# Attention of a two-layer diffusion backbone: heads paired within a key/value head, and single-pass products of split probabilities with split values

## The chip, the cores and the metric

The kernel runs on one core of one Trainium2 chip. The metric is the device time of one execution in microseconds (us); the times given are medians over runs. TensorE is called PE here, VectorE DVE, ScalarE ACT, GpSimd POOL; PEld is TensorE's weight load.

## What is computed

The reference runs two layers over 512 latent tokens and 256 context tokens of width 1024. A layer normalizes, projects, runs three token mixers (attention, pooling, Fourier mixing), gates and sums them, projects again, and ends with a gated MLP. The change is in the attention, which has 8 query heads of width 64 over 2 key/value heads:

```python
def latent_attention(q, k, v, kc, vc, sink):
    qb = q.reshape(B, nb, BLOCK, N_KV_HEADS, Q_PER_KV, HEAD_DIM)
    kb, vb = band(k), band(v)
    s_lat = jnp.einsum('bnqhgd,bnkhd->bhgnqk', qb, kb) * scale
    s_lat = jnp.where(valid, s_lat, NEG_INF)
    s_ctx = jnp.einsum('bnqhgd,bchd->bhgnqc', qb, kc) * scale
    p = jax.nn.softmax(jnp.concatenate([s_lat, s_ctx, sink_column(...)], -1))
    o = (jnp.einsum('bhgnqk,bnkhd->bnqhgd', p_lat, vb)
         + jnp.einsum('bhgnqc,bchd->bnqhgd', p_ctx, vc))
```

A block of 128 latent queries sees its own block of keys and its neighbours, and all 256 context keys; context queries (in the first layer alone) see the context keys. Query head h uses key/value head h // 4.

## The kernel before

All activations lie transposed: channels on the 128 partitions, tokens along the free axis, columns 0 to 511 latent (`LS`), 512 to 767 context (`CS`). Weights come as 128x1024 tiles (`wraw`), which ACT rounds to a float32r part `whi` (L323) and DVE reduces to the rest `wlo` (L324). Every large product is made of three float32r products of 128x128 weights with up to 512 columns (`mmk`, L346), into PSUM banks called `mp` and `mm`.

The attention stage works on a pair of heads `t` (0 to 3) and a block `n` of 128 queries: 24 such units in the first layer (6 blocks, two of them of context queries), 16 in the second. A pair is one head of each key/value head, t and 4 + t, so that its two halves of 64 channels lie on partitions 0 to 63 and 64 to 127. A unit has two halves of code:

- `scores` (L587 to L637): for each head h, PE multiplies the queries with the two parts of the keys (`ka`, `kb`, float32r, 256 or 384 columns, L602 to L607) and adds the masks (L614) in a PSUM tile `sc`; DVE takes the maximum (L617), ACT the exponential into `p` (L627), DVE divides by the sum (L634).
- `pv` (L638 to L662): PE transposes the probabilities in blocks of 128x128 (L649) into the one PSUM bank `tp`, up to four blocks of one head at a time; ACT or DVE, in turn, copies the bank to `pt` (L651, L653). Then each 128-key chunk is multiplied: the weights are 64 columns of the values `vs` in float32, the moving side 128 columns of `pt`, one product for each head at its own column half of the array (`tile_position`, L658), both into one bank `pv`. ACT copies the result to `o` (L662).

A unit has 4 or 5 chunks (latent blocks at the edge, inside) or 2 (context blocks): 160 chunks in all, 88 in the first layer and 72 in the second, so 320 transposes and 320 products at L658; the trace has two records for each of these float32 products, 640.

The kernel is written so that unit n + 1's `scores` comes before unit n's `pv`. After every third unit (second in the second layer) `filler` multiplies one part of the Fourier branch and its gates (L346), work that attention doesn't need. At the middle of the stage the queries of heads t = 2, 3 are projected (`attn_q`). A scheduler then sets each engine's fixed order from this program, so fillers stand between the steps of a unit; engines run their order in sequence and wait on semaphores.

`attn_kv` (L562 to L584) makes the keys' parts and the values: it transposes the values in 128-token chunks (L582) and ACT copies them into the float32 tile `vs` (L583). `SBB` (L36) gives the buffers of the stage's temporary tiles.

Of the kernel before, what the change touches and what calls it, by code (L numbers as in the profile page):

```python
# [35 lines left out]
SBB = dict(p=2, pt=3)  # L36
# [85 lines left out]
class Kern:  # L122
# [52 lines left out]
    def tmp(self, tag, w=N):  # L175
# [7 lines left out]
        return self.tp.tile([P, w], F32, tag=tag, name=tag, bufs=self.sbt[tag])  # L183
# [379 lines left out]
    def attn_kv(self, l, hs, ls, streams):  # L563
# [14 lines left out]
        vs = self.slot(F32)  # L578
        for c0, c1 in (LS, CS):
# [3 lines left out]
            nc.scalar.copy(vs[:, c0 : c1], pv)  # L583
        return ka, kb, vs  # L584

    def scores(self, l, t, n, qs, ka, kb):
# [11 lines left out]
        for h in range(2):  # L598
# [3 lines left out]
            nc.tensor.matmul(cx, q, ka[h][:, T : N], start=True, stop=False)  # L602
            nc.tensor.matmul(cx, q, kb[h][:, T : N], start=False, stop=True)
            if bl:
                bd = s[:, 0:bl]
                nc.tensor.matmul(bd, q, ka[h][:, k0 : k0 + bl], start=True, stop=False)  # L606
                nc.tensor.matmul(bd, q, kb[h][:, k0 : k0 + bl], start=False, stop=False)  # L607
# [30 lines left out]
    def pv(self, st, vs, o):  # L638
        nc = self.nc
        pr, chunks, q0 = st  # L640
        nch = len(chunks)
        pts = []
        for h in range(2):
            pt = self.tmp("pt", 640)
            for j0 in range(0, nch, 4):
                j1 = min(j0 + 4, nch)
                tpb = self.bk("tp", (j1 - j0) * P)
                for j in range(j0, j1):
                    nc.tensor.transpose(tpb[:, (j - j0) * P : (j - j0 + 1) * P], pr[h][:, j * P : (j + 1) * P], self.ident)  # L649
                if (h + j0 // 4) % 2 == 0:  # L650
                    nc.scalar.copy(pt[:, j0 * P : j1 * P], tpb)  # L651
                else:
                    nc.vector.tensor_copy(pt[:, j0 * P : j1 * P], tpb)  # L653
            pts.append(pt)
        po = self.bk("pv", P)
        for j, c in enumerate(chunks):
            for h in range(2):
                nc.tensor.matmul(  # L658
                    po[64 * h : 64 * h + 64, :], vs[:, c * P + 64 * h : c * P + 64 * h + 64],
                    pts[h][:, j * P : (j + 1) * P], start=(j == 0), stop=(j == nch - 1), tile_position=(0, 64 * h),  # L660
                )
        nc.scalar.copy(o[:, q0 : q0 + P], po)  # L662

    def layer(self, l, xs, streams, h=None, after=None):
# [112 lines left out]
        for half in range(2):  # L777
# [3 lines left out]
            for t in ts:  # L781
                for n in range(nblk):
                    st = (self.scores(l, t, n, qs[t], ka, kb), o[t])
# [309 lines left out]
```

## Time and profile before

| | before |
|---|---|
| median of 3 runs | 1896.56 us (1896.4 to 1897.75) |
| span of the profiled execution | 1894.8 us |
| around it (median less span) | 1.8 us |
| PE busy | 1848.8 us, 98% of the span |
| DVE, ACT, POOL busy | 1222.7 us (65%), 679.4 us (36%), 143.2 us (8%) |
| attention, first layer | 205 to 402 us |
| attention, second layer | 1257 to 1399 us |
| granted TensorE clock, both stages | 1.00, which is 2.4 GHz |

The profile is one execution. Busy time is the share in which an engine works on something; PE's records overlap, since a product's end is modelled behind its start, so what a product costs PE is the distance from its start to the next one's start, and not its length. The stages of attention are the stretches in which the names `sc`, `tp`, `pt` and `pv` stand in the trace.

### The profile page before, as it was taken

To read this page: it belongs to the slowest core of one execution; us is meant where nothing else is said; L and a number is where in the kernel's file an instruction comes from. 1 tells how busy PE (TensorE), PEld (TensorE's weight loads), DVE (VectorE), ACT (ScalarE), POOL (GpSimd) and SP (SyncE) were. 2 spreads that over 40 slices of the span, in tenths; PEclk is the share of its full clock that TensorE was granted. 3 is DMA by queue.
4 is the path that set the end of the run, shared out by engine and by line. 5 is a ranking of instruction groups with operands and counts; after the bars stand their busy time and mean duration, and the time that the engine had idled before them with its cause. 6 is when DMAs were issued, how large, how long until landed. Compare 5 with 4: busy or idle time off the path is not lost. (4 is left out here: it accounts for less than half of the span.)

```text
span 1894.8 us, 26908 instructions
## 1 busy us (share of the span) xinstructions
PE 1848.8 (98%) x10584; PEld 1569.8 (83%) x10584; DVE 1222.7 (65%) x2313; ACT 679.4 (36%) x1132; POOL 143.2 (8%) x102
## 2 busy tenths in 40 slices
PE   6999999999999999999999999999999999999997
PEld 4888877788888888888888888877778988888887
DVE  5687655557758995757566676556753776556556
ACT  4332444432234331313232234344443444233333
POOL 2000101012100000000000031010112200000003
PEclk8999999999999999999999999999999999999998
DMA  9244101024542442323233343321123623222233
GB/s 358 90 143 146 46 23 56 23 74 142 169 150 99 147 132 80 122 89 123 89 123 100 111 146 101 104 78 46 51 70 100 203 91 99 95 99 96 99 99 114
DMA packets 75998, 205.09 MB, mean 108 GB/s; under 512 B 8288, under 2 KB 15712, under 8 KB 75744
## 3 DMA queue, kind: packets, MB, share of 16 engines
q1 hardware_dynamic: 75872, 203.38, 33.1%
q8 instruction: 83, 1.36, 0.3%
q14 instruction: 43, 0.35, 0.1%
HBM read 199.15 MB, written 4.19 MB: 107 GB/s over the span
## 5 line engine op out<-in xcount | busy, mean ns | idle before, releaser
L346 PE MATMUL mm<-slot,whi 128*128 128x512 f32 (+1 forms) x3468 | 895.8, 348 | 7.7 <-DVE slot L886 2.7
L346 PEld LDWEIGHTS mm<-slot,whi 128*128 128x128 f32 x3468 | 609.0, 191 | 89.6 <-DVE slot L886 3.1
L346 PE MATMUL mp<-slot,whi 128*128 128x512 f32 (+1 forms) x2404 | 643.8, 353 | 3.0 <-ACT tg L525 1.5
L346 PE MATMUL mm<-slot,wlo 128*128 128x512 f32 (+1 forms) x1734 | 600.2, 346 | 0.0
L346 PEld LDWEIGHTS mp<-slot,whi 128*128 128x128 f32 x2404 | 418.3, 189 | 64.3 <-issue 6.6
L323 ACT CAST whi<-wraw 128x1024 fp32r<-128x1024 f32 x260 | 272.7, 1049 | 539.2 <-PE mm L346 309.4
L324 DVE TENSOR_TENSOR wlo<-wraw,whi 128x1024 fp32r<-128x1024 f32 x245 | 304.3, 1242 | 246.4 <-ACT whi L323 238.7
L346 PE MATMUL mp<-slot,wlo 128*128 128x512 f32 (+1 forms) x1202 | 421.5, 351 | 1.0 <-POOL wlo L324 1.0
L346 PEld LDWEIGHTS mm<-slot,wlo 128*128 128x128 f32 x1734 | 330.9, 191 | 40.1 <-DVE wlo L324 0.6
L346 PEld LDWEIGHTS mp<-slot,wlo 128*128 128x128 f32 x1202 | 227.4, 189 | 31.8 <-issue 4.3
L294 DVE SCALAR_TENSOR_TENSOR junk<-wmod,cb 128x512 f32<-128x512 f32 x256 | 177.4, 693 | 7.8 <-DMA wmod<-in_w_mt_dram 3.8
L886 DVE SCALAR_TENSOR_TENSOR slot<-mm,mod,slot 128x512 f32<-128x512 f32 (+1 forms) x109 | 66.8, 616 | 62.7 <-PE mm L346 62.7
L324 POOL TENSOR_TENSOR wlo<-wraw,whi 128x1024 fp32r<-128x1024 f32 x15 | 36.8, 2455 | 878.8 <-ACT whi L323 878.8
L532 POOL TENSOR_TENSOR slot<-slot,tg 128x512 f32<-128x512 f32 (+1 forms) x48 | 62.2, 1296 | 408.7 <-DVE tg L531 375.8
L835 DVE SCALAR_TENSOR_TENSOR cp<-mm,p,cp 128x511 f32<-128x511 f32 (+2 forms) x122 | 79.2, 650 | 17.5 <-ACT cp L834 15.6
L627 ACT ACTIVATE p<-sc,sm 128x512 f32<-128x512 f32 (+2 forms) x80 | 54.9, 687 | 32.7 <-PE tp L649 21.0
L658 PE MATMUL pv<-pt,slot 128*64 128x128 f32 x640 | 64.3, 283 | 0.4
L834 ACT ACTIVATE cp<-mm,p 128x512 f32<-128x512 f32 (+1 forms) x60 | 36.8, 613 | 57.6 <-PE mm L346 57.6
L617 DVE TENSOR_REDUCE sm<-sc 128x1 f32<-128x512 f32 (+2 forms) x80 | 53.5, 683 | 6.0 <-PE sc L614 6.0
L658 PEld LDWEIGHTS pv<-pt,slot 128*64 128x64 f32 x640 | 41.2, 136 | 17.8 <-issue 8.2
L653 DVE COPY pt<-tp 128x512 f32<-128x512 f32 (+2 forms) x56 | 30.1, 537 | 39.6 <-PE tp L649 39.5
L649 PE MATMUL tp<-p,p 128*128 128x128 f32 x320 | 54.7, 277 | 0.9 <-ACT pt L651 0.9
(157 smaller groups left out, 1323.8 us busy)
## 6 DMA issues: line engine op xcount, KB each, us to landing
wraw<-in_w_up_dram SPq DMA_DIRECT2D x88, 512.0 KB, 3.5
wmod<-in_w_mt_dram SPq DMA_DIRECT2D x160, 256.0 KB, 3.0
wraw<-in_w_in_dram SPq DMA_DIRECT2D x68, 512.0 KB, 3.5
wraw<-in_w_dn_dram SPq DMA_DIRECT2D x56, 512.0 KB, 3.4
wraw<-in_w_out_dram SPq DMA_DIRECT2D x32, 512.0 KB, 3.5
slot<-in_w_m_dram SPq DMA_DIRECT2D x20, 384.0 KB, 7.5
wraw<-in_w_bra_dram SPq DMA_DIRECT2D x8, 512.0 KB, 3.6
slot<-in_xc_dram SPq DMA_DIRECT2D x8, 256.0 KB, 4.5
```

Of the source, the lines that this page charges most:

```text
L294: nc.vector.scalar_tensor_tensor(junk[:, 0:512], w, 1.0, self.cb[:, b, hs], ALU.mult, ALU.mult, accum_out=acc[:, b * 2 + h : b * 2 + h + 1])
L323: self.cpy = nc.scalar.copy(hi, raw)
L324: (eng or nc.vector).tensor_tensor(lo, raw, hi.bitcast(F32), ALU.subtract)
L346: self.mm = self.nc.tensor.matmul(out, ww, xx, start=(k == 0 and i == 0), stop=(k == n - 1 and i == 2))
L532: nc.gpsimd.tensor_tensor(y[:, c0 : c1], y[:, c0 : c1], tg[:, c0:c1], ALU.add)
L617: nc.vector.tensor_reduce(mx[:, h : h + 1], s, AX.X, ALU.max)
L627: nc.scalar.activation(p[:, :w], ps[h], AF.Exp, bias=ngm[:, h : h + 1], scale=0.125, accum_out=den[:, h : h + 1])
L649: nc.tensor.transpose(tpb[:, (j - j0) * P : (j - j0 + 1) * P], pr[h][:, j * P : (j + 1) * P], self.ident)
L658: nc.tensor.matmul(po[64 * h : 64 * h + 64, :], vs[:, c * P + 64 * h : c * P + 64 * h + 64], pts[h][:, j * P : (j + 1) * P], start=(j == 0 ...
L834: nc.scalar.activation(c[:, c0:c1], ps, AF.Copy, scale=cw(1))
L835: tap = lambda d, src, i: nc.vector.scalar_tensor_tensor(c[:, d], src, cw(i), c[:, d], ALU.mult, ALU.add)
L886: nc.vector.scalar_tensor_tensor(xv, ps, g2(m, b), xv, ALU.mult, ALU.add)
```

## The change

Heads are paired as 2t and 2t + 1, which share one key/value head (`t // 2`), so one unit needs one head's values alone. `attn_kv` makes for each key/value head a float32r tile with, per chunk, 128 columns: the values rounded to float32r (64 columns) and the rest (64 columns). `pv` transposes two chunks of both heads at a time into the bank `tp` (512 columns); ACT rounds the bank to `ph` (float32r), and DVE then subtracts that from the bank to get `pl`. A chunk's values are the weights of two products of 256 columns (both heads), one with `ph`, one with `pl`, in one bank of 128 x 256. The two halves of its partitions, the products with the two parts of the values, are added at the end: for each head ACT copies one half to `o` and DVE adds the other.

```diff
-SBB = dict(p=2, pt=3)
+SBB = dict(p=3, ph=2, pl=1)
...
     def attn_kv(self, l, hs, ls, streams):
...
-        vs = self.slot(F32)
+        vs = self.slots(2)
         for c0, c1 in (LS, CS):
...
-            nc.scalar.copy(vs[:, c0 : c1], pv)
+            src = pv.rearrange("p (c d) -> p c d", d=P)
+            for h in range(2):
+                dst = vs[h][:, c0:c1].rearrange("p (c d) -> p c d", d=P)
+                own = src[:, :, 64 * h : 64 * h + 64]
+                nc.scalar.copy(dst[:, :, 0:64], own)
+                nc.vector.tensor_tensor(dst[:, :, 64:P], own, dst[:, :, 0:64].bitcast(F32), ALU.subtract)
...
     def scores(self, l, t, n, qs, ka, kb):
-            nc.tensor.matmul(cx, q, ka[h][:, T : N], start=True, stop=False)
+            nc.tensor.matmul(cx, q, ka[t // 2][:, T : N], start=True, stop=False)
...
     def pv(self, st, vs, o):
         pr, chunks, q0 = st
         nch = len(chunks)
-        pts = []
+        po = self.bk("pv", 2 * P)
+        for j0 in range(0, nch, 2):
+            j1 = min(j0 + 2, nch)
+            w = (j1 - j0) * 2 * P
+            tpb = self.bk("tp", w)
+            for j in range(j0, j1):
+                for h in range(2):
+                    x = ((j - j0) * 2 + h) * P
+                    nc.tensor.transpose(tpb[:, x : x + P], pr[h][:, j * P : (j + 1) * P], self.ident)
+            hi, lo = self.tmp("ph", 512, F32R), self.tmp("pl", 512, F32R)
+            nc.scalar.copy(hi[:, :w], tpb)
+            nc.vector.tensor_tensor(lo[:, :w], tpb, hi[:, :w].bitcast(F32), ALU.subtract)
+            for j in range(j0, j1):
+                v = vs[:, chunks[j] * P : (chunks[j] + 1) * P]
+                x = (j - j0) * 2 * P
+                nc.tensor.matmul(po, v, hi[:, x : x + 2 * P], start=(j == 0), stop=False)
+                nc.tensor.matmul(po, v, lo[:, x : x + 2 * P], start=False, stop=(j == nch - 1))
         for h in range(2):
-            pt = self.tmp("pt", 640)
-            for j0 in range(0, nch, 4):
...
-        po = self.bk("pv", P)
-        for j, c in enumerate(chunks):
-            for h in range(2):
-                nc.tensor.matmul(
-                    po[64 * h : 64 * h + 64, :], vs[:, c * P + 64 * h : c * P + 64 * h + 64],
-                    pts[h][:, j * P : (j + 1) * P], start=(j == 0), stop=(j == nch - 1), tile_position=(0, 64 * h),
-                )
-        nc.scalar.copy(o[:, q0 : q0 + P], po)
+            own, oth = (slice(0, 64), slice(64, P)) if h == 0 else (slice(64, P), slice(0, 64))
+            dst = o[own, q0 : q0 + P]
+            nc.scalar.copy(dst, po[oth, h * P : (h + 1) * P])
+            nc.vector.tensor_tensor(dst, po[own, h * P : (h + 1) * P], dst, ALU.add)
...
-heads = np.array([[t, 4 + t] for t in range(4)]).reshape(-1)
```

On the host the heads' columns in the weights are no longer permuted (the last lines of the diff), which moves no instruction. Outside the attention stages PE, POOL and SP have the same instructions in the same order.

In the first layer, PE's order in the middle of a unit of 5 chunks stood before as below (`tp` transposes, `pv` products with the values, `mp` fillers):

```order
L649 MATMUL tp<-p_87,p 128x128 x4
L346 MATMUL mp<-slot,whi 128x256
L346 MATMUL mp<-slot,wlo 128x256
L346 MATMUL mp<-slot,whi 128x512 x2
L649 MATMUL tp<-p_87,p 128x128
L658 MATMUL pv<-pt,slot 64x128
L346 MATMUL mp<-slot,wlo 128x512
L346 MATMUL mp<-slot,whi 128x512
L649 MATMUL tp<-p_87,p 128x128 x4
```

The same place in the changed program:

```order
L655 MATMUL tp<-p_87,p 128x128 x4
L662 MATMUL pv<-ph,slot 128x256
L663 MATMUL pv<-pl,slot 128x256
L662 MATMUL pv<-ph,slot 128x256
L663 MATMUL pv<-pl,slot 128x256
L655 MATMUL tp<-p_87,p 128x128 x4
L346 MATMUL mp<-slot,whi 128x256 x2
L346 MATMUL mp<-slot,wlo 128x256
```

The products are now of 128 weights and 256 columns, in twos per chunk. In the whole program the 320 products with the values stood in 96 runs between other work of PE: 56 of a single product, 8 of three, 16 of seven and 16 of eight. They now stand in 154 runs, still 320 products.

At the end of the second layer's attention PE's order was:

```order
L649 MATMUL tp<-p_87,p 128x128 x4
L658 MATMUL pv<-pt,slot 64x128
L346 MATMUL mp<-slot,whi 128x512 x2
L346 MATMUL mp<-slot,wlo 128x512
L346 MATMUL mp<-slot,whi 128x512
L658 MATMUL pv<-pt,slot 64x128 x7
L346 MATMUL mp<-slot,whi 128x512
```

It is now:

```order
L655 MATMUL tp<-p_87,p 128x128 x7
L662 MATMUL pv<-ph,slot 128x256
L663 MATMUL pv<-pl,slot 128x256
L662 MATMUL pv<-ph,slot 128x256
L663 MATMUL pv<-pl,slot 128x256
L655 MATMUL tp<-p_87,p 128x128
L662 MATMUL pv<-ph,slot 128x256
L663 MATMUL pv<-pl,slot 128x256
```

The fillers have moved ahead: from the last scores to the stage's end PE now has only transposes (18, of five groups) and products with the values, and the following projections come after the last product.

On DVE, one unit in the middle of the second layer now reads (`pl` is the new subtraction, L668 the new addition, L622 the maximum, L639 the division):

```order
L658 TENSOR_TENSOR pl<-tp,ph 128x256
L622 TENSOR_REDUCE sm_12075<-sc 128x1
L626 SCALAR_TENSOR_TENSOR sm_12090<-sm_12075,nsink 128x2
L668 TENSOR_TENSOR slot<-pv,slot 64x128
L628 TENSOR_TENSOR sm_12092<-sm_12090,nsink 128x2
L658 TENSOR_TENSOR pl<-tp,ph 128x512
L668 TENSOR_TENSOR slot<-pv,slot 64x128
L324 TENSOR_TENSOR wlo<-wraw,whi 128x1024
L658 TENSOR_TENSOR pl<-tp,ph 128x512
```

Before, the same unit had two copies, of 128x128 and of 128x512, where three subtractions and two additions now stand; over the program DVE has 88 subtractions and 80 additions in place of 56 copies, and ACT 88 roundings and 80 copies in place of 96 copies.

## Rows read from the trace of the kernel before

**Rows 1.** The page: busy time of each engine, and the chain that ended last by engine.

```profile
PE 1848.8 (98%) x10584; PEld 1569.8 (83%) x10584; DVE 1222.7 (65%) x2313; ACT 679.4 (36%) x1132; POOL 143.2 (8%) x102
...
PE 27%; DVE 1%; issue 1%; ACT 0%; POOL 0%; POOLq 0%; DVEq 0%; ACTq 0%
```

**Rows 2.** Busy time in the two attention stages: us, then each engine's busy us (instructions).

```profile
205.00:402.00 197.00, 193.08 (x1315) 152.04 (x1313) 113.88 (x270) 86.19 (x219) 19.54 (x18) 1.00 0.11 35
1257.00:1399.00 142.00, 139.96 (x906) 106.08 (x907) 98.12 (x196) 67.24 (x155) 16.62 (x11) 1.00 0.15 48
```

**Rows 3.** PE's waits in the first layer's stage: us in total, times, longest.

```profile
PE mp L346 <- ACT tg L525: 1.5, 6, 0.3
PE sc L602 <- ACT p L627: 1.2, 2, 0.7
```

**Rows 4.** PE's timeline around a single product: start us, length us, what.

```profile
229.86 0.27 PE L649 MATMUL tp<-p,p 128*128 128x128 f32 x1
230.07 0.43 PE L658 MATMUL pv<-pt,slot 128*64 128x128 f32 x2
230.43 0.50 PE L346 MATMUL mp<-slot,wlo 128*128 128x512 f32 x1
230.76 0.39 PE L346 MATMUL mp<-slot,whi 128*128 128x512 f32 x1
```

**Rows 5.** PE's timeline around scores and four transposes.

```profile
227.66 0.28 PE L602 MATMUL sc<-slot 128*128 128x256 f32 x1
227.78 0.28 PE L603 MATMUL sc<-slot 128*128 128x256 f32 x1
227.90 0.28 PE L606 MATMUL sc<-slot 128*128 128x256 f32 x1
...
228.50 0.60 PE L649 MATMUL tp<-p,p 128*128 128x128 f32 x4
228.85 0.48 PE L346 MATMUL mp<-slot,whi 128*128 128x512 f32 x1
229.17 0.39 PE L346 MATMUL mp<-slot,wlo 128*128 128x512 f32 x1
229.40 0.63 PE L346 MATMUL mp<-slot,whi 128*128 128x512 f32 x2
```

**Rows 6.** PE's timeline around a run of eight products (16 records).

```profile
1390.46 0.33 PE L649 MATMUL tp<-p,p 128*128 128x128 f32 x1
1390.72 1.09 PE L658 MATMUL pv<-pt,slot 128*64 128x128 f32 x16
1391.74 0.74 PE L346 MATMUL mp<-slot,whi 128*128 128x512 f32 x2
1392.32 0.39 PE L346 MATMUL mp<-slot,wlo 128*128 128x512 f32 x1
```

**Rows 7.** ACT's and DVE's copies of the transposes, by shape; DVE's small addition nearest in shape.

```profile
L651 ACT COPY pt<-tp 128x512 f32<-128x512 f32 x32 | 18.8, 586 | 48.4 <-PE tp L649 48.3
L651 ACT COPY pt<-tp 128x256 f32<-128x256 f32 x8 | 3.0, 373 | 7.4 <-PE tp L649 7.4
...
L653 DVE COPY pt<-tp 128x512 f32<-128x512 f32 x32 | 22.1, 690 | 28.5 <-PE tp L649 28.4
L653 DVE COPY pt<-tp 128x256 f32<-128x256 f32 x8 | 3.4, 422 | 4.8 <-PE tp L649 4.8
...
L514 DVE TENSOR_TENSOR cp<-aux,st 128x128 f32<-128x128 f32 x3 | 0.9, 286 | 0.0
```

**Rows 8.** Timeline: the copy behind the transposes of rows 5; ACT handing to DVE.

```profile
229.13 0.59 ACT L651 COPY pt<-tp 128x512 f32<-128x512 f32 x1 [1.66 <-PE tp L649]
...
468.99 0.84 ACT L350 CAST slot<-slot 128x768 fp32r<-128x768 f32 x1 [1.69 <-POOL slot L532]
...
469.86 0.96 DVE L351 TENSOR_TENSOR slot<-slot 128x768 fp32r<-128x768 f32 x1 [0.34 <-ACT slot L350]
```

More of the change, by code (lines that the diff above doesn't have):

```diff
@@ L173, in aux, with tmp @@
         return self.bk("aux", w)
-    def tmp(self, tag, w=N):
+    def tmp(self, tag, w=N, dt=F32):
         if tag == "tg":
@@ L182, in tmp @@
             tag = "cv"
-        return self.tp.tile([P, w], F32, tag=tag, name=tag, bufs=self.sbt[tag])
+        return self.tp.tile([P, w], dt, tag=tag, name=tag, bufs=self.sbt[tag])
     def small(self, w):
@@ L601, in scores @@
             cx = s[:, bl:w]
-            nc.tensor.matmul(cx, q, ka[h][:, T : N], start=True, stop=False)
-            nc.tensor.matmul(cx, q, kb[h][:, T : N], start=False, stop=True)
+            nc.tensor.matmul(cx, q, ka[t // 2][:, T : N], start=True, stop=False)
+            nc.tensor.matmul(cx, q, kb[t // 2][:, T : N], start=False, stop=True)
             if bl:
                 bd = s[:, 0:bl]
-                nc.tensor.matmul(bd, q, ka[h][:, k0 : k0 + bl], start=True, stop=False)
-                nc.tensor.matmul(bd, q, kb[h][:, k0 : k0 + bl], start=False, stop=False)
+                nc.tensor.matmul(bd, q, ka[t // 2][:, k0 : k0 + bl], start=True, stop=False)
+                nc.tensor.matmul(bd, q, kb[t // 2][:, k0 : k0 + bl], start=False, stop=False)
                 ms = []
@@ L782, in layer @@
                 for n in range(nblk):
-                    st = (self.scores(l, t, n, qs[t], ka, kb), o[t])
+                    st = (self.scores(l, t, n, qs[t], ka, kb), vs[t // 2], o[t])
                     if prev:
-                        self.pv(prev[0], vs, prev[1])
+                        self.pv(*prev)
                     prev = st
@@ L789, in layer @@
                         filler()
-            self.pv(prev[0], vs, prev[1])
+            self.pv(*prev)
         for _ in range(8):
@@ L1044, in _layout @@
             poolw[o : o + 64, l, g // 2, o : o + 64] = i["pool_w"][l, g]
-    heads = np.array([[t, 4 + t] for t in range(4)]).reshape(-1)
-    sink = np.broadcast_to(i["attn_sink"][:, heads].reshape(1, 16), (P, 16))
+    sink = np.broadcast_to(i["attn_sink"].reshape(1, 16), (P, 16))
     a["pk2"] = np.concatenate(
@@ L1064, in _layout @@
     a["w_brp"], a["w_brf"] = two(i["w_br_pool"]), two(i["w_br_four"])
-    wa = tile_m(i["w_br_attn"][:, qp], 4, 8)
+    wa = tile_m(i["w_br_attn"], 4, 8)
     a["w_bra"] = wa.reshape(NL, 4, 2, P, 4, P).transpose(0, 1, 3, 2, 4, 5).reshape(NL, 4, P, 1024)
```

12 lines of the change are left out of this document (1 added, 11 removed).

## The prediction

> **What bounds the kernel now.** The page comes first: PE is busy for 98% of the span and holds 27 of the 30% of the span that the chain of waits names [rows 1]. What changes lies in two stages, so I read those alone. In both PE is busy for 98% of the stretch, DVE for 58% and 69% [rows 2], and PE's list of waits over the first stage's 197 us holds 2.7 us in these two lines [rows 3]. So both stages last as long as PE's own list of work, and the first question is what that list gets shorter by. The second is whether DVE and ACT still deliver in time when it is shorter.
>
> **What a product with the values costs PE today.** I read distances between starts. Take a single product, in two records: from the transpose at 229.86 to the second filler at 230.76 are 0.90 us [rows 4]. In them lie one transpose and one 512-column filler. That filler costs 0.23 elsewhere (229.17 to 229.40), and four transposes with one filler take 0.67 (228.50 to 229.17), so a transpose costs 0.11 [rows 5]. The single product is left with 0.56 us. Its two records account for 0.22 at a transpose's rate, so 0.34 is a fixed toll of going into this kind of product and out again. For a run of eight (16 records) from 1390.46 to 1392.32 are 1.86 us; less one transpose and two fillers that is 1.29 [rows 6]. There two records, one of each column half, go at a time. A run of three then costs 0.34 + 4 x 0.11 = 0.78; runs of seven have one unpaired product and I price them as runs of eight.
>
> The order has 56 runs of one, 8 of three, 32 of seven or eight: 31.4 + 6.2 + 41.3 = **78.9 us**, of which 44.8 fall to the first layer (32, 8 and 16 runs) and 34.1 to the second (24 and 16).
>
> **What it costs afterwards.** 320 products of 128 weights and 256 float32r columns, the shape of the scores, whose starts lie 0.12 apart [rows 5]: 320 x 0.12 = **38.4 us**. I charge no toll on entering them, because a filler behind transposes pays none: 4 x 0.11 + 0.23 is all that rows 5 leave. The transposes are the same 320. PE's list shortens by **40.5 us**, 23.7 in the first layer and 16.8 in the second.
>
> The Trainium skill, page TensorEngine Tiling (Array Packing), section Key Properties, speaks against the change: different column tiles work in parallel. By that rule alone, with a chunk's four records in 4 x 0.11 / 2 = 0.22 us, 160 chunks cost 35.2 us before and 38.4 afterwards, and the sum would be 3 us slower; rows 6 show the pairing, rows 4 show that 56 products have no partner beside them and that each run pays 0.34.
>
> **What is added elsewhere.** DVE loses 56 copies (30.1 us; 25.5 of them in the two larger shapes [rows 7]). It gets 88 subtractions from PSUM, 72 of 512 and 16 of 256 columns, at the copies' 0.69 and 0.42 [rows 7]: 56.4 us. It also gets 80 additions of 64 x 128 at the 0.29 of the nearest small operation on PSUM [rows 7]: 22.9 us. Net 49, split by chunks 27 and 22. The stages' DVE work goes from 114 and 98 us [rows 2] to 141 and 120. Against stages of 197 - 24 = 173 and 142 - 17 = 125 us that is 81% and 96%: DVE is no longer idle enough to be ignored. ACT gets 88 roundings and 80 copies for 96 copies, some 20 us in the first stage: 106 of 173. The values' preparation in `attn_kv` adds four DVE and two ACT operations per layer of under half a microsecond each; the first scores and the fillers ahead of the first products hide them, and without that cover it would be 2 us.
>
> **What the new hand-overs cost.** There is still one bank `tp`, and a group of transposes is now read by ACT, then by DVE, before PE may write the next. From a group's first transpose to ACT's start are 0.63 us (228.50 to 229.13), ACT takes 0.59, the hand-over to DVE 0.03 (469.83 to 469.86), DVE 0.69, and PE is back 0.14 after a copy's end (229.72 to 229.86) [rows 4, 5, 7, 8]: **2.08 us** for four transposes with idle queues, 1.37 for two. What stands in PE's order within that time hides it.
>
> At the end of the second layer's attention nothing does: five groups (four of four, one of two) take 4 x 2.08 + 1.37 = 9.7 us, and PE has 18 transposes and 18 products for it, 4.1 us. It waits **5.6 us**. Before, fillers stood there, as the order shows.
>
> Elsewhere I went along the new order with these prices and wrote down how much less than the need stands between a group and the product or transpose that waits for it. Most loops hold 2 to 4 us of PE work and cover it. Where the order excerpt shows four transposes, four products and four transposes again, 0.92 us stand against 2.08, and the products themselves wait. All such places together make **9.1 us**.
>
> The last term is unknown: a subtraction may find DVE at other work. At 82% busy and 0.42 us a DVE instruction (113.88 / 270 [rows 2]), a chance arrival waits 0.17; on ACT, 0.6 x 0.39 / 2 = 0.11. Counted along the same order, 0.28 us more on each group lengthens PE's list by 10.6 us, about 43% of 88 x 0.28, because the rest finds cover. Bounds: 0 where the subtractions meet an idle DVE, as most copies do now, and 18 us where DVE's queue makes the delay half a microsecond. I take **7**, nearer the chance arrival, since DVE's order puts most of the subtractions between short instructions.
>
> **Sum.** -40.5 + 5.6 + 9.1 + 7 = -18.8 us. The profiled execution has a span of 1894.8 and some 1.8 around it, which is the median of the runs, 1896.56; the forecast is 1896.6 - 18.8 = **1878 us**. A measurement of this kernel can tell a change of about 0.2%, 4 us, from none.
>
> **Rivals.**
>
> *DVE's and ACT's queues become the bound; slower.* Its place is the bank `tp`, one group after another. Each 0.1 us of mean delay per group costs PE 3.8 us at first and over 4 later on; with 14.7 us already gone to waits, the gain is used up at about 0.6 us of delay, and at 0.66, where the waits come to 45 us, the time is **1901**. For it: in the second stage 96% of DVE would be needed at PE's pace. It has additions that wait for ACT's copies ahead of subtractions that PE waits for, and today's tolls on PE give DVE and ACT time that disappears. Against it: a stage that waits gets longer, so DVE's share falls (at 137 us to 88%), which limits the delay; and today DVE sits idle for 28.5 us ahead of its 32 larger copies [rows 7], so most of them find it free. 10%. The Trainium skill, same page, section PSUM Bottleneck, states this case: more speed on TensorE does not speed up emptying PSUM, which can become the limit. No row of the kernel before shows that limit reached.
>
> *The toll stays.* If the 0.34 us came with the change of bank or operand rather than with column halves, 154 runs would pay 52 us, and the products would cost 91: 12 us more than now, **1909** before any wait. Transposes and score products change bank and operand too and pay nothing [rows 5], so 3%. The same section Key Properties has a rule on this side: a change of tiling mode drains the array; by it the toll goes.
>
> *All hand-overs covered but the tail.* Then 40.5 - 5.6 = 34.9 us are won: **1862**. For it: PE's list of waits is short today [rows 3]. Against: the copies there are one step, not two. 17%.
>
> *Won and lost in equal parts,* with 0.5 to 0.65 us of delay per group and a time within 4 us of today's. 8%.
>
> The forecast, a gain of 8 to 30 us, has 62%. The range from 1862 to 1898 leaves out most of the two slower rivals and half of the full gain. Faster: 62 + 17 = 79%; the same 8%; slower 13%.
>
> **What would show it.** In the trace of the changed kernel: products with the values 0.12 apart with no gap behind transposes (else the toll stays); `tp` bank cycles near 2.1 us and PE waiting at the new subtraction's products by 10 to 25 us over the two stages; the first stage 10 to 16 us shorter, the second 3 to 9; DVE near 77% and 88% of the stages; the tail of the second layer with PE idle about 6 us. The forecast is wrong if a stage is longer than before, if PE waits under 8 us or over 35, or if time moves outside the two stages.

## The result, and the profile after

The changed kernel takes **1912.1 us** (median of 4 runs, 1910.9 to 1913.7) against 1896.9 for the kernel before on the same chip: ratio 1.0078, 95% interval 1.0064 to 1.0093. It is 15.2 us slower where 18.8 us less were forecast, and outside the range. The profiled execution has a span of 1912.0 us; it is the longest of the four (1913.7), so its parts below add up to a little more than 15.2.

From the page of the changed kernel, busy time and the chain by engine (beside [rows 1]):

```profile
PE 1844.2 (96%) x10264; PEld 1575.5 (82%) x10264; DVE 1266.9 (66%) x2433; ACT 711.0 (37%) x1208; POOL 146.3 (8%) x102
...
PE 30%; DVE 2%; issue 1%; ACT 1%; POOL 0%; POOLq 0%; DVEq 0%; ACTq 0%
```

PE's share falls from 98% to 96%, and the chain names DVE with 2% and ACT with 1%, where it had 1% and 0%. To see where the time went I use one row of each run: the sequencer's event at the line that scales the output projection (the line behind both attentions, L816 before, L822 after; 26 times, first and last start). Before and after:

```profile
L816 DVEq EVENT_SEMAPHORE  x26: 21/21/21, 520.9 to 1511.6; - x26
```

```profile
L822 DVEq EVENT_SEMAPHORE  x26: 21/21/21, 524.9 to 1528.3; - x26
```

The first stands behind the first layer's attention and comes 4.0 us later, the last behind the second layer's and comes 16.7 us later. So the first layer's attention costs 4.0 us more and the second's 12.7 more. The same row gives this split for every run below; it is one profiled execution each, to be read to about 2 us.

The two stages of the changed kernel (columns as in [rows 2]; the stretches are as long as the stages have become):

```profile
205.00:412.00 207.00, 192.40 (x1189) 159.95 (x1188) 142.43 (x333) 105.35 (x259) 24.24 (x19) 0.99 0.11 36
1262.00:1416.00 154.00, 143.76 (x783) 111.42 (x781) 113.19 (x242) 81.39 (x187) 15.03 (x11) 0.95 0.16 50
```

PE was busy for 98 and 99% of the stages before and is for 93% now. DVE is at 69% and 73%, below the 77% and 88% that I had expected: it is not full. PE's list of waits over the whole span:

```profile
PE mp L346 <- ACT tg L525: 5.2, 5, 2.0
PE tp L655 <- DVE pl L658: 5.1, 5, 1.4
...
PE pv L663 <- DVE pl L658: 3.4, 5, 1.3
PE pv L662 <- ACT ph L657: 3.4, 5, 0.9
PE sc L607 <- ACT p L632: 3.0, 6, 0.9
```

These are waits that [rows 3] did not have, on DVE's subtraction (L658) and ACT's rounding (L657), but as a list they are far from the 34 us between the forecast and the measurement (18.8 + 15.2): the list counts time in which no record lies on PE, and a product's record covers the start of the wait behind it. The groups of the new instructions say more:

```profile
L658 DVE TENSOR_TENSOR pl<-tp,ph 128x512 fp32r<-128x512 f32 (+1 forms) x88 | 56.2, 638 | 28.6 <-ACT ph L657 28.0
L655 PE MATMUL tp<-p,p 128*128 128x128 f32 x320 | 56.0, 281 | 5.7 <-DVE pl L658 5.1
L657 ACT CAST ph<-tp 128x512 fp32r<-128x512 f32 (+1 forms) x88 | 47.9, 544 | 30.6 <-PE tp L655 30.0
```

88 subtractions take 56.2 us, as forecast, but DVE stands idle 28 us ahead of them, waiting for ACT, and ACT 30 us ahead of its roundings, waiting for PE, and PE waits for DVE before it writes the bank again. Ahead of these operations the three engines wait for one another in turn.

The prices of the forecast hold where nothing waits. PE's timeline in the second layer (start us, length us):

```profile
1310.61 0.39 PE L662 MATMUL pv<-ph,slot 128*128 128x256 f32 x1
1310.83 0.28 PE L663 MATMUL pv<-pl,slot 128*128 128x256 f32 x1
1310.94 0.28 PE L662 MATMUL pv<-ph,slot 128*128 128x256 f32 x1
1311.06 0.28 PE L663 MATMUL pv<-pl,slot 128*128 128x256 f32 x1
1311.18 0.27 PE L655 MATMUL tp<-p,p 128*128 128x128 f32 x1
```

Products start 0.11 to 0.12 us apart, the first after 0.22. And a cycle of the bank `tp`, in the timeline of all engines at the end of the second layer:

```profile
1400.22 0.60 PE L655 MATMUL tp<-p,p 128*128 128x128 f32 x4
...
1400.86 0.58 ACT L657 CAST ph<-tp 128x512 fp32r<-128x512 f32 x1 [0.17 <-PE tp L655]
...
1401.48 0.69 DVE L658 TENSOR_TENSOR pl<-tp,ph 128x512 fp32r<-128x512 f32 x1 [0.22 <-ACT ph L657]
...
1402.22 0.90 PE L655 MATMUL tp<-p,p 128*128 128x128 f32 x3 [1.40 <-DVE pl L658]
```

From the first transpose to the next write are 2.00 us; 2.08 were priced. So neither a product nor one hand-over was mis-sized. What was, the experiments had to tell.

### The profile page after: what moved, and what is told of

The parts are those of the page before. It is cut to its first block, busy times and chain, and to the rows that moved or that the text cites. A ratio compares the mean times of both kernels' runs of the same rounds, so it can differ in the third digit from the quotient of the medians.

```text
span 1912.0 us, 26520 instructions
## 1 busy us (share of the span) xinstructions
PE 1844.2 (96%) x10264; PEld 1575.5 (82%) x10264; DVE 1266.9 (66%) x2433; ACT 711.0 (37%) x1208; POOL 146.3 (8%) x102
## 5 line engine op out<-in xcount | busy, mean ns | idle before, releaser
L294 DVE SCALAR_TENSOR_TENSOR junk<-wmod,cb 128x512 f32<-128x512 f32 x256 | 177.7, 694 | 6.4 <-DMA wmod<-in_w_mt_dram 2.5
L658 DVE TENSOR_TENSOR pl<-tp,ph 128x512 fp32r<-128x512 f32 (+1 forms) x88 | 56.2, 638 | 28.6 <-ACT ph L657 28.0
L657 ACT CAST ph<-tp 128x512 fp32r<-128x512 f32 (+1 forms) x88 | 47.9, 544 | 30.6 <-PE tp L655 30.0
L662 PE MATMUL pv<-ph,slot 128*128 128x256 f32 x160 | 52.1, 330 | 4.8 <-ACT ph L657 3.4
L622 DVE TENSOR_REDUCE sm<-sc 128x1 f32<-128x512 f32 (+2 forms) x80 | 53.8, 677 | 0.5 <-PE sc L619 0.3
```

The costliest lines, as they stand in the source:

```text
L294: nc.vector.scalar_tensor_tensor(junk[:, 0:512], w, 1.0, self.cb[:, b, hs], ALU.mult, ALU.mult, accum_out=acc[:, b * 2 + h : b * 2 + h + 1])
L622: nc.vector.tensor_reduce(mx[:, h : h + 1], s, AX.X, ALU.max)
L658: nc.vector.tensor_tensor(lo[:, :w], tpb, hi[:, :w].bitcast(F32), ALU.subtract)
L662: nc.tensor.matmul(po, v, hi[:, x : x + 2 * P], start=(j == 0), stop=False)
```

## The experiments

My first theory after reading the two traces was the tail of the second layer: there PE idles among the last groups, and the granted clock reads 0.50 from 1405 to 1420 us. The rival was that the two-step hand-over (ACT, then DVE, on the one bank `tp`) costs time everywhere in the stages. In the table, times are medians, differences are to the kernel before on the same chip, and the columns by layer come from the row shown above, in one profiled execution of each run.

| run | us | difference | first layer | second |
|---|---|---|---|---|
| changed kernel | 1912.1 | +15.2 | +4.0 | +12.7 |
| e3_no_sub | 1876.0 | -20.8 | -13.4 | -6.1 |
| e16_group_before | 1871.4 | -25.7 | -16.6 | -5.8 |
| e9_load_only | 1880.1 | -17.0 | -10.9 | -6.2 |
| e10_bank_held | 1895.2 | -2.0 | +0.3 | +2.9 |
| e4_no_add | 1905.5 | +8.6 | -0.7 | +9.2 |
| e7_tail_work | 1911.8 | +15.0 | +5.3 | +10.0 |
| e8_gate_ahead | 1911.2 | +14.4 | +3.6 | +11.6 |
| e5_full_cols | 1899.8 | +2.6 | -0.1 | +2.9 |
| e11_pool_scale | 1984.7 | +87.6 | +41.7 | +48.4 |
| e12_two_banks | 1899.8 | +2.7 | -1.0 | +4.7 |
| e13_two_banks_late | 1903.6 | +6.5 | -1.8 | +8.2 |
| e14_two_banks_pool | 1895.5 | -2.4 | +2.2 | -3.7 |
| e15_pool_gate | 1894.2 | -3.7 | +2.3 | -3.1 |

Each difference holds more than the edit that is shown, because the scheduler makes the order anew for every program. By the traces only e7_tail_work and e8_gate_ahead keep the changed kernel's order on PE, but for what they move. In the other runs made from the changed kernel some 400 to 730 of PE's instructions in each attention stage stand at other places. Fillers show it best. Behind the last score product of the second layer 44 of them stand in the kernel before and none in the changed kernel; in e3, e9 and e16 they are 45, 44 and 47, in e10, e11 and e14 24, in e15 33, in e4, e12 and e13 none. So a difference between two rows is what the edit brings together with the order made for it.

### The subtraction taken out

```diff
-            nc.vector.tensor_tensor(lo[:, :w], tpb, hi[:, :w].bitcast(F32), ALU.subtract)
...
-                nc.tensor.matmul(po, v, lo[:, x : x + 2 * P], start=False, stop=(j == nch - 1))
+                nc.tensor.matmul(po, v, hi[:, x : x + 2 * P], start=False, stop=(j == nch - 1))
```

> The changed kernel without the subtraction that makes pl; the second product of each chunk multiplies ph again, so the low part of the probabilities is left out. PE keeps its 320 transposes and 320 products of 256 columns, DVE loses 88 instructions, and the bank tp is free when ACT's rounding ends, so a group's way from its first transpose to the next write is 0.63 + 0.59 + 0.14 = 1.4 us where it was 2.1. Theory (the two-step hand-over through the single bank tp, ACT and then DVE, eats what the products save): 1862 to 1882 us, faster than the kernel before. Rival 1 (the products themselves, or entering them, cost more than 0.12 us each): 1900 or more, since they are all still there. Rival 2 (the additions at the end of a unit hold the bank pv and DVE): 1895 or more.

1876.0 us, ratio 0.9892 (0.9877 to 0.9907): as the theory had it. With every product and transpose in place the kernel is 20.8 us faster than before, and 36.0 faster relative to the changed kernel. Products that cost more than priced cannot be the cause.

### The additions taken out

```diff
-            nc.vector.tensor_tensor(dst, po[own, h * P : (h + 1) * P], dst, ALU.add)
```

> The changed kernel without the 80 additions at the end of a unit: ACT still copies one half of the bank pv, and the half that DVE would add is left out of the result. DVE loses some 20 us of work in the two stages, the subtractions keep their place. Theory (the hand-over through tp is the cause): 1898 to 1910 us, still slower than the kernel before. Rival (the additions hold pv and come ahead of subtractions in DVE's queue): 1890 or less.

1905.5 us: the additions are worth 6.6 us, the subtractions 36.

### The tail, with unused work and with work held back

```diff
...
+            if idle:
+                with self.after(tr):
+                    ps = self.bk("sc", 1024)[:, 0:512]
+                    for i in range(5):
+                        nc.tensor.matmul(ps, idle[i][:, 0:P], idle[i + 1][:, 0:512], start=(i == 0), stop=(i == 4))
...
```

> The changed kernel with 25 more products on PE, 128x128 by 512 columns, whose result nobody reads: five behind each of the five groups of transposes at the end of the second layer's attention; no other instruction changes its place. At the 0.23 us of a filler they are 5.7 us more work for PE. Theory (PE stands idle there for the hand-overs, the granted clock then falls to one half, and the half clock stretches the chain and the projections behind it): the granted clock stays at 1.00 from 1400 to 1420 us, and the time falls by 2 to 6 us against the changed kernel, to 1906 to 1910. Rival (the tail is bound by ACT and DVE alone and the clock costs nothing, or falls all the same): no change or up to 5 us more, 1911 to 1917.

1911.8 us, no change, where the first theory had 1906 to 1910. Windows of the changed kernel and of this run in the tail (the clock is the number behind POOL's):

```profile
1400.00:1405.00 5.00, 2.87 (x14) 2.25 (x14) 2.14 (x7) 2.56 (x7) 0.00 (x0) 0.61 0.00 0
...
1410.00:1415.00 5.00, 3.25 (x11) 2.11 (x10) 1.66 (x3) 1.17 (x2) 0.00 (x0) 0.50 0.01 2
1415.00:1420.00 5.00, 3.62 (x9) 2.79 (x10) 1.27 (x3) 1.14 (x3) 0.00 (x0) 0.50 0.09 26
```

```profile
1400.00:1405.00 5.00, 2.85 (x10) 2.15 (x11) 2.78 (x8) 1.97 (x6) 0.00 (x0) 0.77 0.00 0
...
1410.00:1415.00 5.00, 4.63 (x25) 3.33 (x24) 2.54 (x8) 1.65 (x5) 0.00 (x0) 1.00 0.00 0
1415.00:1420.00 5.00, 3.44 (x16) 2.57 (x15) 1.96 (x4) 1.26 (x4) 0.00 (x0) 1.00 0.10 31
```

In both the clock falls in the first stretch, where PE is busy for 2.9 of 5 us. With more products among the groups it is back at 1.00 (2.4 GHz) from 1410 on, where it was 0.50 (1.2 GHz). The last score product, the rounding of the second group and the first product of the next step, in the changed kernel (with two groups' transposes) and in this run (with the first five unused products):

```profile
1398.49 0.23 PE L619 MATMUL sc<-maskb,identb 128*128 128x128 bf16 x1
...
1404.29 0.58 ACT L657 CAST ph<-tp 128x512 fp32r<-128x512 f32 x1 [1.66 <-PE tp L655]
...
1408.95 1.21 PE L655 MATMUL tp<-p,p 128*128 128x128 f32 x4
...
1412.41 1.05 PE L655 MATMUL tp<-p,p 128*128 128x128 f32 x4
...
1417.31 1.19 PE L346 MATMUL mm<-slot,whi 128*128 128x512 f32 x2 [1.38 <-DVE slot L668]
```

```profile
1399.23 0.23 PE L619 MATMUL sc<-maskb,identb 128*128 128x128 bf16 x1
...
1403.33 2.50 PE L660 MATMUL sc<-slot 128*128 128x512 f32 x5
...
1406.90 0.59 ACT L662 CAST ph<-tp 128x512 fp32r<-128x512 f32 x1 [3.53 <-PE tp L655]
...
1417.89 0.70 PE L346 MATMUL mm<-slot,whi 128*128 128x512 f32 x2 [1.38 <-DVE slot L673]
```

Score product and next step are 18.8 and 18.7 us apart, but the equal sum hides two parts. The first five unused products run at the half clock and stand between the second group's transposes, so its rounding starts 7.7 us behind the score product where it started 5.8. From there to the next step are 11.0 us where they were 13.0. So the half clock costs about 2 us of this tail, and the unused work costs as much: the run has the rival's number by a balance, and shows only that the clock is far too small for the whole loss. The other edit holds useful work back:

```diff
...
+            if l and half:
+                wa = self.weights("w_bra", l, 0)
+                with self.after(self.last):
+                    early = self.in_tile(l, 26, hs, ls, streams)
             self.pv(*prev)
...
```

> The changed kernel with the first gate product of the step behind the attention of the second layer (24 products of 512 columns, L346) held back until the last scores are on PE; the changed kernel's order has them spread over the last four units. Same work, 24 products moved into the tail. Theory (the tail without other work costs 12 of the 15 us that were lost): PE has 5.5 us of work among the last five groups, the granted clock stays up, and the time falls by 4 to 9 us, to 1903 to 1908. Rival (the loss is one of waits everywhere in the stages, so cover taken from the units before costs as much there as it brings in the tail): 1910 to 1915.

1911.2 us: the rival's number. In the trace 33 fillers now stand behind the last score product. PE waits there for some 7.6 us where it waited 14.5, an estimate from the distances, with 0.11, 0.12 and 0.23 us for a transpose, a product and a filler. But from the second layer's first score product to its last are 137.5 us (1260.72 to 1398.27) where they were 136.9 (1261.56 to 1398.49), though the 33 fillers, 7.6 us, have left this stretch: the units before lose that cover. With the hand-overs as they are, PE's other work is worth the same at either place in the second layer. In the first layer no run tests this.

### What the subtraction costs: load, bank, or wait

The first of these keeps DVE's 88 subtractions but lets them read `ph` alone, and no product reads `pl` (both edits below); the second has the lower edit alone, so that DVE reads the bank as in the changed kernel.

```diff
-            nc.vector.tensor_tensor(lo[:, :w], tpb, hi[:, :w].bitcast(F32), ALU.subtract)
+            nc.vector.tensor_tensor(lo[:, :w], hi[:, :w].bitcast(F32), hi[:, :w].bitcast(F32), ALU.subtract)
...
-                nc.tensor.matmul(po, v, lo[:, x : x + 2 * P], start=False, stop=(j == nch - 1))
+                nc.tensor.matmul(po, v, hi[:, x : x + 2 * P], start=False, stop=(j == nch - 1))
```

> DVE's load alone: the 88 subtractions stay in DVE's order at the same size, but take ph from both sides, so they read no bank and nobody reads pl; the second product multiplies ph again, so the low part of the probabilities is left out. DVE is as busy as in the changed kernel; the bank tp is free when ACT has read it, and no product waits for DVE. It stands between the run without subtractions (1876.0 us) and the changed kernel (1912.1). Theory (the loss is the length of the hand-over: the bank held until DVE has read it, and the second product that waits for DVE): 1876 to 1884 us. Rival (the loss is DVE's load, which delays the maxima, divisions and additions as well): 1896 or more.

> The subtractions read the bank tp as in the changed kernel, so the bank is held until DVE is done, but nobody reads pl; the second product multiplies ph again, so the low part of the probabilities is left out. Against the run with DVE's load alone this adds the held bank, against the changed kernel it lacks the products' wait for pl. Theory (the single bank, held through two steps, is the larger part): 1892 to 1908 us. Rival (the products' wait for pl is the larger part): 1876 to 1890 us.

1880.1 us (ratio 0.9905, 0.9890 to 0.9920) and 1895.2 us (0.9992, 0.9981 to 1.0002). With the run above and the changed kernel they make a ladder, from -20.8: DVE's load adds **3.8** us, the bank held until DVE has read it **15.0**, the products' wait for `pl` **17.2**, and that is +15.2. DVE's load is as good as free. Both other steps belong to one thing, the time from PE's transposes through ACT and DVE and back. How the 32.2 us divide between them is less sure: the ten executions of the second run lie between 1889.9 and 1898.6 us, and its trace is of one at 1898.3. Its median lies in its theory's range, but that the bank is the larger part, as that theory had it, isn't shown. The last step also holds DVE's wait for the one tile `pl`, until the products have read it. And the orders differ, as said: behind the second layer's last score product PE waits, by the estimate above, 2.7 us with 44 fillers, then 6.2 with 24, then 14.5 with none. The run with 24 gate products held back, which keeps the order otherwise, speaks against the place of the fillers as the cause in the second layer; for the first the ladder alone stands. In the group of subtractions of the first of the two, DVE's idle time ahead of them:

```profile
L658 DVE TENSOR_TENSOR pl<-ph 128x512 fp32r<-128x512 f32 (+1 forms) x88 | 60.5, 687 | 6.6 <-ACT ph L657 6.4
```

DVE works more here (60.5 us), and waits 6.4 us for ACT where it waited 28.0: ACT's roundings are mostly done when DVE comes to its turn.

### The products, without their wait for the rounding

In place of `pl` this run has a third tile `ph`.

```diff
...
             nc.scalar.copy(hi[:, :w], tpb)
+            use, wu = self.held or (hi, w)
+            self.held = hi, w
...
+                x = x % wu
+                nc.tensor.matmul(po, v, use[:, x : x + 2 * P], start=(j == 0), stop=False)
...
```

> The run without subtractions (1876.0 us), with each group's products multiplying the rounded tile ph of the group before, which has long been there, so that no product waits for its own group's hand-over (the result is computed from the wrong blocks of probabilities, and without their low part). The products, transposes, roundings and additions are as many, and the bank tp is still handed over. It tells what became of the 40.5 us that PE's list was to lose, of which the run without subtractions shows 20.9. Theory (the list is 40 us shorter, and the rest goes to products that wait for the rounding, with a weight load that cannot run ahead): 1858 to 1868 us. Rival (the products cost more than 0.12 us each wherever they stand, or the rest of the stage does): 1872 to 1878.

1871.4 us (ratio 0.9862, 0.9846 to 0.9879): between the theory's range and the rival's, 4.9 us less than without the subtraction alone. PE's timeline of this run:

```profile
267.96 0.60 PE L655 MATMUL tp<-p,p 128*128 128x128 f32 x4
268.32 0.36 PE L664 MATMUL pv<-ph,slot 128*128 128x256 f32 x1
268.52 0.28 PE L665 MATMUL pv<-ph,slot 128*128 128x256 f32 x1
268.64 0.28 PE L664 MATMUL pv<-ph,slot 128*128 128x256 f32 x1
268.76 0.28 PE L665 MATMUL pv<-ph,slot 128*128 128x256 f32 x1
268.88 0.39 PE L346 MATMUL mp<-slot,whi 128*128 128x512 f32 x1
```

Four transposes and four products in 0.92 us, which is 4 x 0.11 + 4 x 0.12 as priced. Still only 25.7 of the 40.5 us of PE's list arrive. By the distances between starts over all runs of products, with the waits right before and behind them, the products take 82 us before, where 78.9 were priced, and 49 here, where 38.4 were. The bank that ACT hands back, and the scores that wait for `p`, are left in this run; how the remaining 14.8 us divide among them was not taken apart.

### Column halves

```diff
-        po = self.bk("pv", P)
-        for j, c in enumerate(chunks):
-            for h in range(2):
+        po = self.bk("pv", 2 * P)
+        for h in range(2):
+            for j, c in enumerate(chunks):
                 nc.tensor.matmul(
...
+                    po[:, h * P : (h + 1) * P], vs[:, c * P : (c + 1) * P], pts[h][:, j * P : (j + 1) * P],
...
```

> The kernel before with one part changed: its pairing, its float32 values and its copies of whole transposes stay, but a product has all 128 columns of the values as weights, for one head after the other, into a bank of 256 columns, and ACT copies the useful half for each head. No column halves, 320 float32 products of two records each, 0.22 us at a transpose's rate, 70.4 us in all, in 100 runs. Theory (the 0.34 us of each run of products at column halves were a toll of the column halves): 8 us less than the 78.9 us of the kernel before, 1886 to 1892 us. Rival (the 0.34 us are paid by whatever product first meets the values' weights or a wait there, halves or not): 70.4 + 100 x 0.34 = 104 us, 1910 to 1925.

1899.8 us (ratio 1.0015, 1.0006 to 1.0025): neither. Its timeline, a single product and a run of eight:

```profile
225.77 0.49 PE L658 MATMUL pv<-pt,slot 128*128 128x128 f32 x2
226.01 0.36 PE L346 MATMUL mp<-slot,wlo 128*128 128x256 f32 x1
...
235.78 2.11 PE L658 MATMUL pv<-pt,slot 128*128 128x128 f32 x16
237.64 0.36 PE L602 MATMUL sc<-slot 128*128 128x256 f32 x1
```

A single product takes 0.24 us with all columns and took 0.56 with halves [rows 4], so the toll of 0.34 us is one of the column halves, as I had read it. But eight take 1.86 against 1.29 [rows 6], since pairs no longer run side by side: 56 singles would win 0.32 each, 18 us, but the 16 runs of eight would lose 0.57 each and the 16 of seven, at 0.23 a product, some 0.3. By these rows 320 products take 320 x 0.23 = 74 us, not my 70.4, against 78.9. The order differs too: 100 runs, 20 of them of a single product. By the distances over all of these runs, waits beside them included, the products take 83 us where they took 82, so the 5 us gained by price did not arrive.

### DVE relieved, and a way to a faster kernel

```diff
-            nc.vector.tensor_scalar(pr[h][:, :w], pr[h][:, :w], rc[:, h : h + 1], None, ALU.mult)
+            nc.gpsimd.tensor_scalar(pr[h][:, :w], pr[h][:, :w], rc[:, h : h + 1], None, ALU.mult)
```

> The changed kernel with the division of the probabilities (L639, 80 instructions of 0.48 to 0.54 us on DVE for the larger shapes, some 40 us over the two stages) on POOL, which is 8% busy and takes 1.56 us for an addition of 512 columns. Rival of the run with DVE's load alone (DVE's load is the bound): 1895 to 1906 us, since DVE loses nearly as much as the subtractions brought. Theory (the length of the hand-overs is the bound, and DVE's share in it only its own two steps): no gain over the changed kernel, 1908 to 1925, since the probabilities come 1 to 2 us later.

1984.7 us, far beyond both. The division takes POOL 1.9 us where DVE takes 0.54, and the transposes wait for it:

```profile
L639 POOL TENSOR_SCALAR p<-p,sm 128x640 f32<-128x640 f32 x32 | 60.9, 1916 | 44.6 <-ACT ph L657 39.2 <-DVE sm L637 4.2 <-PE sc L619 0.8
```

```profile
PE tp L655 <- POOL p L639: 61.3, 62, 2.6
```

It agrees with the chain as the bound (a longer step on it costs, though POOL is otherwise mostly idle), and as a test of DVE's load it is spoilt by that length.

```diff
...
-        self.phase(dict(sc=2, tp=1, pv=1), SBB)
+        self.phase(dict(sc=2, tp=2), SBB)
...
+        po = self.bk("sc", 1024)[:, 768:1024] if po is None else po
...
+                        self.pv(*prev, po)
...
```

> The changed kernel, whole result, with two banks tp in place of one, and two tiles pl: the products' sums move from the bank pv into 256 unused columns of the next unit's scores bank, which frees a bank. (A scratch tile of an earlier stage is made bfloat16 to find the room for the second pl.) DVE's and ACT's work is the same. Theory (the single bank, held through two steps, costs the 15 us between the runs with DVE's load alone and with the bank held): a group's transposes no longer wait for DVE's step of the group before; 10 to 18 us less than the changed kernel, 1894 to 1902. Rival (a second bank only moves the wait to the products that need pl, which cost 17 us of their own): 1904 to 1914.

The run has two tiles `pl` as well as two banks, so it doesn't tell the two apart; the scratch tile in bfloat16 changes no time that its trace shows (0.69 us for each of its instructions, L294, in both).

And with the second products later in the program:

```diff
...
+            while len(late) > (2 if j1 < nch else 0):
+                v, x = late.pop(0)
+                nc.tensor.matmul(po, v, x, start=False, stop=(j1 == nch and not late))
...
```

> As the run with two banks, and the products with pl stand behind the next group's transposes and its products with ph in the program, so that DVE's step has a group's time before PE needs it. Whole result. Theory (held bank and the wait for pl together are the 32 us between the run with DVE's load alone, 1880.1, and the changed kernel): most of them come back, 1878 to 1890 us, which would beat both kernels. Rival (PE's fixed order puts other waits in their place, since each unit is still one chain through ACT and DVE and the tail of the second layer has no other work): 1895 to 1908.

1899.8 us with two banks: 12.5 us of the loss come back, within the theory's range. With the second products later as well it is 1903.6, the rival's number; why that order does harm was not taken apart. What waits next in the run with two banks is the scores, for the additions (L669) that read the sums in their bank:

```profile
PE sc L608 <- DVE slot L669: 6.0, 8, 1.4
```

So the additions left DVE in the last two runs, the second of which also holds back the gate products, by the edit shown above:

```diff
...
+            if h == 0:
+                pa = self.tmp("pa", P)
             nc.scalar.copy(dst, po[oth, h * P : (h + 1) * P])
-            nc.vector.tensor_tensor(dst, po[own, h * P : (h + 1) * P], dst, ALU.add)
+            nc.scalar.copy(pa[own, :], po[own, h * P : (h + 1) * P])
+            nc.gpsimd.tensor_tensor(dst, pa[own, :], dst, ALU.add)
...
```

> As the run with two banks (1899.8 us), with the 80 additions taken from DVE: ACT copies both halves of a unit's sums out of the bank and POOL adds them from there. Whole result. ACT gets 80 more copies of 0.26 us, DVE loses 80 additions of 0.29, and the scores bank that holds the sums comes free after ACT's copies, without a turn in DVE's queue: in the run with two banks PE waited 6.0 us for those additions, and without additions the changed kernel was 6.7 us faster. Theory (what is left of the loss is time in DVE's queue): 6 to 14 us less, 1886 to 1894 us, faster than both kernels. Rival (ACT, which is also in every hand-over, takes DVE's place): 1897 to 1904.

> As the run with two banks and the additions on POOL, and 24 gate products (L346, 512 columns) of the following step held back until the second layer's last scores are on PE, as in the run that did this to the changed kernel and brought nothing there. Whole result. Theory (with shorter hand-overs the units before the tail can do without that cover, and the tail cannot): 1 to 5 us less than the run without it. Rival (cover is worth the same wherever it stands): within 1 us of it.

1895.5 us (ratio 0.9986, 0.9976 to 0.9996), between the theory's range and the rival's, and 1894.2 us (0.9977, 0.9967 to 0.9988). The last is 0.2% faster than the kernel before, which just can be measured, and 1% faster than the changed kernel. Moving the additions was to give 6 to 14 us against the run with two banks and gave 5, and a row of its waits on PE says why:

```profile
PE sc L608 <- ACT pa L671: 9.8, 29, 0.7
```

The scores now wait for ACT's copies in the same bank, a wait that the borrowed place of the sums brought in. Holding back the gate products is worth 1.3 us here, in the theory's range but too little to be told from nothing; and the edit moves little, since 24 fillers stand behind the last scores without it and 33 with it.

## Why the prediction was wrong, step by step

**What bounds the kernel now** was right for the kernel before. The first sentence behind it, that the stages get shorter as PE's list does, holds for as long as the hand-overs fit beside the list.

**The toll of the column halves and the price of the new products** were right: 0.24 against 0.56 for a product with and without halves, 0.92 for four transposes and four products. The rival that the toll stays is out; that its 1909 us lies nearest to 1912.1 is chance. "PE's list shortens by 40.5 us" is right by these prices and wrong as a gain: 25.7 arrive where no product waits, 20.8 with ACT's step in the way.

**What the new hand-overs cost** is the step that failed. I had 2.08 us for a cycle, and 2.00 were measured; I had 5.6 + 9.1 + 7 = 21.7 us for all that it would leave uncovered. With 15.2 us lost where 40.5 were to be gained, 55.7 us went elsewhere, into waits as far as is known: 14.8 that were not taken apart, 4.9 with the products' wait for ACT's rounding, and 36.0 with DVE's step, 32.2 of them by the held bank and the wait for `pl` (each with the order made for its run). The tail of the second layer holds 14.5 of them (below); so what stands elsewhere, 9.1 + 7 in the forecast, came to some 41, an estimate that takes the 14.8 as waits. The forecast had named more than 35 us of waits as a sign of being wrong. Two assumptions made it small. "Most loops hold 2 to 4 us of PE work and cover it" took PE's other work as cover for each group by itself. But shortening PE's list takes cover away, and what covers one group is missing at another; in the second layer holding 24 products back for the tail brought nothing. "About 43% of 88 x 0.28, because the rest finds cover" has the same fault. The sum had to be made the other way round as well: the length of one unit's way through PE, ACT and DVE, in their order, against the time per unit. From the last score product to the next step, through the last two units, are 18.8 us in the changed kernel, and that is not 9.7.

The Trainium skill, page TensorEngine Tiling (Array Packing), section PSUM Bottleneck, advises using both ScalarE and VectorE to empty PSUM. Here it matters in what order they do it: the kernel before had them side by side on different transposes; one after the other on the same bank, by the ladder above, cost 15.0 us for the bank and 17.2 for the wait.

**The rivals.** The first one has the direction and the place (the single bank `tp`); I gave it 10% and 1901 us, and it came to 1912. Its mechanism, that steps queue because DVE and ACT are full, is not what happened: DVE's share fell to 69% and 73%, and its load alone costs 3.8 us. It is the length of the way through both: an engine that is 30% idle can still be the one that is waited for, when it must come second. That "all hand-overs are covered but the tail" had 17% and is the farthest off.

**The tail** got 5.6 us of idle PE in the forecast, and this term was mis-sized too. Behind the last score product 18 transposes and 19 products, 4.3 us by their prices, stand in 18.8 us, so PE waits 14.5. The term counted five cycles of the bank. It left out 1.7 us before the first group (until 1400.22) and 1.8 behind the last product (1415.52 to 1417.31). It also left out that the products with `pl` stand ahead of the next transposes: between the last two groups are 3.46 us and not 2.08. The half clock, not foreseen, has a part in that, about 2 us over the whole tail. Filling the tail still won nothing, as the held-back products show. Of the signs that the forecast named, the spacing of the products and the bank's cycle came; the stages were to be 10 to 16 and 3 to 9 us shorter, and cost 4.0 and 12.7 more (by the names in the trace they are 10 and 12 longer, with 51 and 23 more fillers in them).

## What to carry to other kernels

When a change replaces work on the busiest engine by a longer hand-over through other engines, price the loop as well as the list: how long one unit takes from engine to engine and back, how many are in flight (here one, since there is one bank), and compare that with the shortened time per unit. Idle time on the engines of the loop is no cover; an operand split into two parts is cheap in load and dear in latency when the second part needs the first. Taking the step out, keeping its load alone, and keeping its bank alone, three runs, told load from latency. Where a scheduler makes the order anew for each of them, compare the orders as well as the times.

## What was not expected of the hardware

In the rows below, a product whose semaphore comes late pays for its weights too. In the changed kernel's timeline (PEld is the weight load), a product without and one with such a wait:

```profile
228.73 0.28 PE L662 MATMUL pv<-ph,slot 128*128 128x256 f32 x1
228.85 0.28 PE L663 MATMUL pv<-pl,slot 128*128 128x256 f32 x1
228.87 0.24 PEld L655 LDWEIGHTS tp<-p,p 128*128 128x128 f32 x2
228.97 0.38 PE L655 MATMUL tp<-p,p 128*128 128x128 f32 x2
...
230.21 0.19 PEld L607 LDWEIGHTS sc<-slot 128*128 128x128 f32 x1 [0.38 <-ACT p L632]
230.22 0.39 PE L607 MATMUL sc<-slot 128*128 128x256 f32 x1
...
230.44 0.28 PE L608 MATMUL sc<-slot 128*128 128x256 f32 x1
```

The transposes' load runs 0.10 us ahead of them, beside the product before, and that product takes 0.12. The score product that waited starts with its own load, and the next comes 0.22 behind it: 0.10 us on top of the wait (the run with unused work shows the same at its tail, 1398.51 to 1398.73). The Trainium skill, page TensorE: Matmul & The Clock Gate, section Architectural detail: the array is 16× 32×32, not 1× 128×128, says that PE's queue can pull a weight load ahead of products in flight; the rows at 228.87 agree, and those at 230.21 show a case in which it does not. What this toll makes over all waits was not measured by itself.
